# Hybrid RG-LRU / attention block: the first two chunk pairs of the MLP's first product as eight plain products each, sums of squares off POOL

## Chip, core and metric

One core of a Trainium2 chip runs the whole program in one launch. The metric is device time in microseconds, the median of three runs.

## What is computed

A transformer block on 512 tokens of width 1024, in float32: RMS norm, a fused input projection, a gated linear recurrence (RG-LRU) beside differential attention, a gated merge, and then the part that matters here:

```python
x = x + merged @ w_out[l]
h2 = rms_norm(x, norm2_g[l])
x = x + jnp.square(jax.nn.relu(h2 @ w_mlp1[l])) @ w_mlp2[l]
return rms_norm(x, normf_g)
```

w_mlp1 is 1024 x 4096, w_mlp2 is 4096 x 1024.

## The kernel before

**Layout and precision.** Activations lie transposed, 128 features on the partitions and 512 tokens along a row. A float32 product is made of three float32r products: each operand is split into a rounded part ("hi") and the remainder ("lo"), and hi*hi, hi*lo and lo*hi are summed in PSUM. A split is a cast on ScalarE (ACT) and a subtraction on VectorE (DVE): `part` (L132, L133) for whole weight chunks, `split_to` (L191 to L193) for everything in the MLP.

**w_out (L710 to L739).** Eight products, one for each 128 output features, of 24 matmuls with 512 columns (`mm`, L163 to L165), in the order m = 0, 4, 1, 5, 2, 6, 3, 7 (`OUT_ORDER`); n counts them. After each, DVE adds the residual (L719, tile E) and scales by the gain (L722, tile V; halves m and m+4 of a pair k = m % 4 lie in one tile), ACT squares (L724, L727) and POOL adds the squares to `ssq` (L728). The token mean itself is not applied to the activation: it is folded into x2 (L752) and into the final norm, so that the MLP need not wait for it.

**The MLP's first product.** It is cut into four quarters q of the hidden width, each of four chunk pairs i: one unit `("one", q, i)` makes hidden features i and i + 4 of quarter q (256 in all) for all 512 tokens. A unit is a 2 x 2 block product (input features in halves, tokens in halves of 256), done with seven products in place of eight (the Strassen-Winograd scheme): `one` (L777 to L799) uses the activation quarters b11, b21, b22 and four combinations t1 to t4, and seven weight pieces, four of which are sums of raw weight blocks (L206 to L211, DVE). Each of the seven products is 12 matmuls of 256 columns (`mm4`, L237) into one of four half banks BX, BY, BR, BZ. DVE and ACT read these partial results in between (L785, L787, L789, L791, L793, L795, L797); then `f_split` (L766) squares the relu and splits it into the tiles V and B (q even) or R and Q (q odd).

The activation combinations t1 to t4 are formed for each k when m = k + 4 is done (L734 to L738: two subtractions, one addition, one subtraction, then a split of 1024 columns), and the plain quarters b11 (tiles S0, S1) and b21, b22 (tiles L) are split there too.

**The MLP's second product.** Units `("two", q, i)` (L801) take two output features m of the hidden quarter q: 48 matmuls with 512 columns, added to x2 by L808.

**Order.** The four units (one, 0, 0..3) come first, alone; then `one` of the next quarter and `two` of this one alternate (`mlp_order`, L69). Weight pieces pass through a ring of eight (`RING`, L168): `use(n)` (L228) makes the split of piece n + 7 before it hands out piece n, and 2, 4, 6 and 8 of them are asked for during and behind w_out (L713, L740). SP loads one unit's raw weights (1 MB) ahead (`load_unit`, L185, two buffers). The framework sets the order in which each engine takes its instructions before the program runs, by dependences and the program's order; on an engine it isn't always the program's. Behind w_out also stand the token sums (`token_sums`, L329, on PE), a few small DVE instructions (L743 to L748), a broadcast on PE (L336), its copy on ACT (L340) and the scaling of x2 (L752, four of 128 x 1024).

Of the kernel before, what the change touches and what calls it, by code (L numbers as in the profile page):

```python
# [9 lines left out]
FR = mybir.dt.float32r  # L10
AF = mybir.ActivationFunctionType
ALU = mybir.AluOpType
AX = mybir.AxisListType

P = 128
T = 512
# [3 lines left out]
NQ = 4  # L20
# [17 lines left out]
H2 = T // 2  # L38
# [30 lines left out]
def mlp_order():  # L69

    order = [("one", 0, i) for i in range(4)]
    for q in range(NQ):
        for i in range(4):
            if q + 1 < NQ:
                order.append(("one", q + 1, i))
            order.append(("two", q, i))
    return order


def merge_order():  # L80
# [8 lines left out]
class Build:  # L89
# [12 lines left out]
    def t(self, tag, shape=(P, T), dt=F, bufs=1):  # L102
        self.n += 1
        return self.sb.tile(list(shape), dt, tag=tag, name=f"{tag}_{self.n}", bufs=bufs)

    def ps(self, tag, shape=(P, T), bufs=1):
        self.n += 1
        return self.pp.tile(list(shape), F, tag=tag, name=f"p{tag}_{self.n}", bufs=bufs)
# [61 lines left out]
    def plan_pieces(self):  # L170
        self.units = mlp_order()
        self.pieces = []
        self.first = []
        for u, (kind, q, i) in enumerate(self.units):
            self.first.append(len(self.pieces))
            if kind == "one":
                self.pieces += [(u, j) for j in range(7)]
            elif q < NQ - 1:
                self.pieces += [(u, j) for j in range(4)]
        self.ring_h, self.ring_l = [], []  # L180
        self.piece, self.made = {}, 0
        self.raw_u = {}
        self.sums = {}
# [11 lines left out]
    def make_piece(self):  # L195
        V, n = self.nc.vector, self.made
        u, j = self.pieces[n]
        self.load_unit(u)
        self.load_unit(u + 1)
        raw = self.raw_u[u]  # L200
        blk = [raw[:, i] for i in range(4)]
        if self.units[u][0] == "one":

            if j == 0:
                s1 = self.sums[u] = self.t("pT", (P, T))
                V.tensor_tensor(s1, blk[2], blk[3], op=ALU.add)  # L206
                V.tensor_tensor(blk[2], blk[2], blk[0], op=ALU.add)
            elif j == 1:
                V.tensor_tensor(blk[0], blk[0], self.sums[u], op=ALU.add)
            elif j == 6:  # L210
                V.tensor_tensor(blk[1], blk[1], blk[0], op=ALU.add)  # L211
            src = (blk[0], blk[0], blk[2], self.sums[u], blk[1], blk[3], blk[1])[j]
        else:
            src = blk[j]
        s, e = n // 2 % (self.RING // 2), n % 2
        if n < self.RING and e == 0:
            self.ring_h.append(self.t("whi", (P, 2, T), FR, bufs=4))
            self.ring_l.append(self.t("wlo", (P, 2, T), FR, bufs=4))
        hi, lo = self.ring_h[s][:, e], self.ring_l[s][:, e]
        self.split_to(src, hi, lo)  # L220
        self.piece[n] = [x.rearrange("p (k m) -> p k m", m=P) for x in (hi, lo)]
        self.made += 1
# [6 lines left out]
        self.make_until(n + self.RING)  # L229
        return self.piece.pop(n)  # L230

    def mm4(self, out, w, xs, first, last):

        nc = self.nc
        for k, (xh, xl) in enumerate(xs):
            for g, (l, r) in enumerate(((w[0], xh), (w[0], xl), (w[1], xh))):
                nc.tensor.matmul(out, l[:, k], r, start=(first and k == 0 and g == 0),  # L237
                                 stop=(last and k == 3 and g == 2), skip_group_check=True)

    def proj(self, xh, xl):  # L240
# [7 lines left out]
def block_kernel(ctx: ExitStack, tc: tile.TileContext, a):  # L248
    nc = tc.nc
    b = Build(tc, ctx, a)  # L250
    b.cur = 0
    t, ps = b.t, b.ps
    V, A, TE = nc.vector, nc.scalar, nc.tensor
# [39 lines left out]
    last = [None]  # L293
# [12 lines left out]
    def col(off, i):  # L306
        return sm[:, off + i:off + i + 1]
# [25 lines left out]
    def bcast_rinv(r, out, sl=range(4)):  # L333
        pb = ps("tr", (P, T))
        for i in sl:
            TE.matmul(pb[:, i * P:(i + 1) * P], r[:, i:i + 1].to_broadcast([P, P]), ident, start=True, stop=True)  # L336
        if out is None:
            return pb
        s = slice(sl[0] * P, (sl[-1] + 1) * P)
        A.copy(out[:, s], pb[:, s])  # L340

    def pair(tag):
        p = t(tag, (P, 2, T), FR)
        return p[:, 0], p[:, 1]
# [11 lines left out]
    ssq = t("up1")  # L356
# [12 lines left out]
    for half in range(2):  # L369
        for kp in range(4):  # L370
# [7 lines left out]
            for kk in range(2):  # L378
                k = 2 * kp + kk
# [23 lines left out]
                for n, (xs, wi) in enumerate(((xh, 0), (xl, 0), (xh, 1))):  # L403
                    for q, i in todo:
                        TE.matmul(pvs[half][i], xs[q][:, i * P:(i + 1) * P], (hv, lv)[wi][:, q % 2],  # L405
                                  start=(q == 0 and n == 0), stop=(q == KT - 1 and n == 2))
# [217 lines left out]
    for j in range(KT // 2):  # L624
        for n in range(8):
            s = 8 * j + n
            p_ = b.proj(xh, xl)
            h = 2 * j + n // 4
# [74 lines left out]
    x2, x2p = [None] * KT, [None] * (KT // 2)  # L703
    th = [t(f"X{2 * k}", (P, 4, H2), FR) for k in range(4)]
    tl = [t(f"X{2 * k + 1}", (P, 4, H2), FR) for k in range(4)]
    b2h = [t(f"L{k}", (P, 2, T), FR) for k in range(2)]
    b2l = [t(f"L{k + 2}", (P, 2, T), FR) for k in range(2)]
    b1h, b1l = t("S0", (P, 4, H2), FR), t("S1", (P, 4, H2), FR)
    ssq = t("up1")
    for n, m in enumerate(OUT_ORDER):  # L710
        k = m % 4
        if n > 4:
            b.make_until(2 * (n - 4))  # L713
        if x2p[m // 2] is None:
            x2p[m // 2] = t(f"E{m // 2}", (P, 2, T))
        xk = x2[m] = x2p[m // 2][:, m % 2]
        nc.sync.dma_start(xk, a["xT"][m])
        po = b.proj(mh, ml)
        V.tensor_tensor(xk, po, xk, op=ALU.add)  # L719
        if m < 4:  # L720
            xs = t(f"V{k}", (P, 2, T))
        V.scalar_tensor_tensor(xs[:, m // 4], xk, col(C_G2, m), r1b, op0=ALU.mult, op1=ALU.mult)  # L722
        if n == 0:
            A.activation(ssq, xk, AF.Square)  # L724
        else:
            sq = t("tmp", bufs=2)
            A.activation(sq, xk, AF.Square)  # L727
            nc.gpsimd.tensor_tensor(ssq, ssq, sq, op=ALU.add)  # L728
        if m >= 4:

            q4 = xs.rearrange("p a (c f) -> p (a c) f", c=2)
            b.split_to(q4[:, 0], b1h[:, k], b1l[:, k])

            tt = t(f"B{k}", (P, 4, H2))  # L734
            V.tensor_tensor(tt[:, 0:3:2], q4[:, 0:2], q4[:, 1:4:2], op=ALU.subtract)
            V.tensor_tensor(tt[:, 1], tt[:, 0], q4[:, 3], op=ALU.add)
            V.tensor_tensor(tt[:, 3], q4[:, 2], tt[:, 1], op=ALU.subtract)
            b.split_to(tt, th[k], tl[k])  # L738
            b.split_to(xs[:, 1], b2h[k // 2][:, k % 2], b2l[k // 2][:, k % 2])  # L739
    b.make_until(b.RING)  # L740
    pc = token_sums([ssq])
# [4 lines left out]
    eps4 = t("eps4", (P, 4))  # L746
    V.tensor_tensor(eps4, sig2, sig2, op=ALU.mult)
    V.tensor_scalar(eps4, eps4, EPS, None, op0=ALU.mult)  # L748
    sg2b = t("up0")
    bcast_rinv(sig2, sg2b)  # L750
    for xp in x2p:
        V.tensor_tensor(xp, xp, sg2b.unsqueeze(1).to_broadcast([P, 2, T]), op=ALU.mult)  # L752


    xc = {
        "b11": [(b1h[:, k], b1l[:, k]) for k in range(4)],
        "b21": [(b2h[k // 2][:, k % 2, :H2], b2l[k // 2][:, k % 2, :H2]) for k in range(4)],
        "b22": [(b2h[k // 2][:, k % 2, H2:], b2l[k // 2][:, k % 2, H2:]) for k in range(4)],
    }
# [4 lines left out]
    fq = {q: [None] * KT for q in range(NQ)}  # L764

    def f_split(q, f, z, lo_half):  # L766
        if q % 2 == 0:
            hi, lo = pair(f"V{f}" if f < 4 else f"B{f - 4}")
        else:
            hi, lo = pair(f"R{f}" if f < 4 else f"Q{f - 4}")  # L770
        A.activation(z[:, lo_half:], z[:, lo_half:], AF.Relu)
        A.activation(hi, z, AF.Square)
        A.activation(z, z, AF.Square)
        V.tensor_tensor(lo, z, hi.bitcast(F), op=ALU.subtract)
        fq[q][f] = (hi, lo)

    def one(u, q, i):  # L777
        n = b.first[u]
# [21 lines left out]

    def two(u, q, i):  # L801
        n = b.first[u]
        for c in range(2):
            m = 2 * i + c
            pz = ps("mm", bufs=3)
            for h in range(2):
                b.mm4(pz, b.use(n + 2 * c + h), fq[q][4 * h:4 * h + 4], h == 0, h == 1)
            V.tensor_tensor(x2[m], pz, x2[m], op=ALU.add)  # L808
# [15 lines left out]

    held = 0
    for u, (kind, q, i) in enumerate(b.units):
        if kind == "one":
            one(u, q, i)
        elif q < NQ - 1:
            two(u, q, i)  # L830
            if q == NQ - 2 and i >= 2:
                hold(len(b.units) - 4 + held, held)
                held += 1
# [5 lines left out]
    ssq = t("up1")  # L839
    for half in range(2):  # L840
        s = slice(half * H2, (half + 1) * H2)
        for m in range(KT):
            hi, lo = last_chunks[m]
            pz = ps("mm", bufs=3)
# [4 lines left out]
            sq = t("tmp", bufs=2)  # L849
# [5 lines left out]
        c = slice(2 * half, 2 * half + 2)  # L855
# [6 lines left out]
        for m, w in ((0, 1), (1, 1), (2, 2), (4, 2), (6, 2)):  # L862
            xp = x2p[m // 2][:, m % 2:m % 2 + w, s]
# [75 lines left out]
```

## Time and profile before

| | us |
|---|---|
| median of three runs | 908.75 (908.32 to 909.1) |
| the profiled execution | 908.68 |
| its span | 906.9 |
| PE busy | 885.7 (98%) |
| DVE busy | 597.1 (66%) |
| ACT busy | 477.5 (53%) |
| POOL busy | 11.7 (1%) |

The span is from the first to the last instruction; 1.8 us lie around it. PE is TensorE's matmuls, PEld its weight loads, which overlap them; matmuls are pipelined, so the recorded duration of one overlaps that of the next, and the pace is read from start to start. The same holds for DVE: in a dense run the starts of 512-wide instructions stand closer than their durations say. Some matmul records can be missing. The granted clock is a share of full speed: 1.00 is 2.4 GHz and 0.50 is 1.2 GHz. psc and pmm are tiles of PSUM; X, S, L, V, B, E, R and Q are tiles of SBUF as above; whi and wlo are the weight ring.

### The profile page before, as it was taken

Reading aid. Unit: us, or ns where it says so; the run is one execution under the profiler, and the core shown is the slowest. Engines: PE = TensorE matmul, PEld = TensorE weight load, DVE = VectorE, ACT = ScalarE, POOL = GpSimd, SP = SyncE. Lnnn points to the kernel's source line nnn. Section 1 sums busy time; section 2 is a strip of 40 time slices with the busy share of each in tenths; the row PEclk is TensorE's granted clock in tenths of the full one; section 3 lists DMA queues with packets and bytes.
Section 4 is the critical chain, followed back from the end, with each engine's and each line's share of the span. In section 5 each row is a group of like instructions: output and inputs, shape, how many; then the busy total and the mean of one; then the engine's idle time right before and its main releaser. Section 6 shows DMA issues by size and latency. Waiting matters only on the chain.

```text
span 906.9 us, 12306 instructions
## 1 busy us (share of the span) xinstructions
PE 885.7 (98%) x4793; PEld 741.9 (82%) x4793; DVE 597.1 (66%) x1008; ACT 477.5 (53%) x863; POOL 11.7 (1%) x12
## 2 busy tenths in 40 slices
PE   9999999999999999999999987999999999999996
PEld 7887777777877788888888877888888888888996
DVE  7767697787787765333334998776666666665633
ACT  7634767857758974222223344664444444445532
POOL 0000000000000000000000210000000000000000
PEclk9999999999999999999999978999999999999998
DMA  8443123133222112222522211222333222233211
GB/s 295 145 134 112 58 70 128 59 111 100 93 83 92 43 53 91 93 94 93 186 93 93 94 47 47 94 94 94 101 115 110 93 93 94 94 102 124 100 48 46
DMA packets 20745, 88.58 MB, mean 98 GB/s; under 512 B 3024, under 2 KB 6352, under 8 KB 11728
## 3 DMA queue, kind: packets, MB, share of 16 engines
q1 hardware_dynamic: 20688, 87.81, 28.3%
q8 instruction: 37, 0.61, 0.3%
q14 instruction: 20, 0.16, 0.1%
HBM read 81.51 MB, written 2.10 MB: 92 GB/s over the span
## 4 chain that ended last, share of the span: by engine, by line
PE 92%; DVE 5%; ACT 2%; issue 1%; POOLq 0%; DVEq 0%; ACTq 0%
PE pmm L237 20%; PE psc L237 17%; PE pmm L163 14%; PE pmm L165 14%; PE pmm L164 14%; PE pmm L405 3%; PE psc L405 2%; PE psc L493 2%; PE pmm L528 2%; PE ptr L516 1%; DVE wlo L193 1%; DVE V L722 1%; PE psc L589 1%; ACT whi L192 1%; PE ptr L336 1%
## 5 line engine op out<-in xcount | busy, mean ns | idle before, releaser
L192 ACT CAST whi<-raw 128x512 fp32r<-128x512 f32 (+1 forms) x148 | 90.5, 629 | 135.6 <-PE psc L237 59.3
L132 ACT CAST whi<-raw 128x1024 fp32r<-128x1024 f32 (+1 forms) x76 | 76.3, 1006 | 130.9 <-PE pmm L164 121.4
L163 PE MATMUL pmm<-X,whi 128*128 128x512 f32 x328 | 132.4, 404 | 0.0
L164 PE MATMUL pmm<-X,whi 128*128 128x512 f32 x328 | 130.1, 397 | 0.0
L165 PE MATMUL pmm<-X,wlo 128*128 128x512 f32 x328 | 130.0, 396 | 0.0
L133 DVE TENSOR_TENSOR wlo<-raw,whi 128x1024 fp32r<-128x1024 f32 (+1 forms) x76 | 89.5, 1179 | 60.0 <-ACT whi L132 59.4
L193 DVE TENSOR_TENSOR wlo<-raw,whi 128x512 fp32r<-128x512 f32 (+1 forms) x148 | 103.7, 709 | 33.3 <-ACT whi L192 30.7
L237 PE MATMUL psc<-X,whi 128*128 128x256 f32 x512 | 99.2, 292 | 1.7 <-ACT tmp L785 1.0
L237 PEld LDWEIGHTS psc<-X,whi 128*128 128x128 f32 x512 | 81.3, 194 | 7.6 <-DVE rot L791 2.0
L163 PEld LDWEIGHTS pmm<-X,whi 128*128 128x128 f32 x328 | 61.7, 188 | 18.1 <-issue 2.6
L165 PEld LDWEIGHTS pmm<-X,wlo 128*128 128x128 f32 x328 | 61.7, 188 | 15.0
L164 PEld LDWEIGHTS pmm<-X,whi 128*128 128x128 f32 x328 | 61.8, 188 | 14.3 <-issue 0.4
L237 PE MATMUL psc<-X,wlo 128*128 128x256 f32 x256 | 71.4, 286 | 0.0
L237 PE MATMUL psc<-L,whi 128*128 128x256 f32 x256 | 51.0, 294 | 7.1 <-DVE tmp L787 7.1
L237 PEld LDWEIGHTS psc<-L,whi 128*128 128x128 f32 x256 | 39.9, 191 | 13.6 <-DVE tmp L787 10.1
L237 PEld LDWEIGHTS psc<-X,wlo 128*128 128x128 f32 x256 | 48.8, 194 | 0.0
L297 ACT ACTIVATE B<-psc,nb 128x128 f32<-128x128 f32 (+3 forms) x64 | 33.2, 523 | 26.8 <-DVE nb L498 23.9
L297 ACT ACT_TABLE_LOAD x32 | 41.1, 1283 | 1.1 <-DVE nb L498 0.5
L237 PE MATMUL pmm<-V,whi 128*128 128x512 f32 x128 | 41.6, 396 | 0.0
L237 PE MATMUL pmm<-B,whi 128*128 128x512 f32 x128 | 40.0, 394 | 0.0
L237 PE MATMUL psc<-L,wlo 128*128 128x256 f32 x128 | 36.3, 283 | 0.0
L237 PE MATMUL pmm<-R,whi 128*128 128x512 f32 (+1 forms) x128 | 32.2, 335 | 0.0
(306 smaller groups left out, 1858.7 us busy)
## 6 DMA issues: line engine op xcount, KB each, us to landing
raw<-wts SPq DMA_DIRECT2D x70, 1024.0 KB, 4.8
rot<-B SPq DMA_DIRECT2D x64, 64.0 KB, 2.0
L<-xT SPq DMA_DIRECT2D x8, 256.0 KB, 5.3
raw<-wts SPq DMA_DIRECT2D x8, 256.0 KB, 5.3
E<-xT SPq DMA_DIRECT2D x8, 256.0 KB, 5.2
out<-E SPq DMA_DIRECT2D x6, 256.0 KB, 2.5
tmp<-gates SPq DMA_DIRECT2D x8, 128.0 KB, 4.6
out<-E SPq DMA_DIRECT2D x4, 128.0 KB, 1.9
```

What stands on the lines that cost most here:

```text
L132: nc.scalar.copy(hf[:, s], raw[:, s])
L133: nc.vector.tensor_tensor(lf[:, s], raw[:, s], hf[:, s].bitcast(F), op=ALU.subtract)
L163: nc.tensor.matmul(ps, hi[:, k], xh[k], start=(k == 0), stop=False)
L164: nc.tensor.matmul(ps, hi[:, k], xl[k], start=False, stop=False)
L165: nc.tensor.matmul(ps, lo[:, k], xh[k], start=False, stop=(k == KT - 1))
L192: self.nc.scalar.copy(hi, src)
L193: self.nc.vector.tensor_tensor(lo, src, hi.bitcast(F), op=ALU.subtract)
L237: nc.tensor.matmul(out, l[:, k], r, start=(first and k == 0 and g == 0), stop=(last and k == 3 and g == 2), skip_group_check=True)
L297: ins = A.activation(*args, **kw).ins
L405: TE.matmul(pvs[half][i], xs[q][:, i * P:(i + 1) * P], (hv, lv)[wi][:, q % 2], start=(q == 0 and n == 0), stop=(q == KT - 1 and n == 2))
L493: TE.matmul(sc[:, m, :n], l[rows, 0, i * P:n], r[rows, 1, :n], start=(g == 0), stop=(g == 2))
L528: TE.matmul(po[:, i], pdT[:, j], v[j][:, h * P:(h + 1) * P], start=(j == 0), stop=(j == i))
```

## The change

The units (one, 0, 0) and (one, 0, 1) are done with eight plain products instead of seven: `one_plain` multiplies the four raw weight blocks with the activation quarters b11, b12, b21 and b22 (b12 is split for it, tiles B0 and B1), into whole banks "mm", two halves of 256 columns each, of which the first matmul alone clears the bank. These two units have four weight pieces each and no weight sums. The combinations t1 to t4 move into `combine(k)`, called twice behind each of the two units. The sums of squares run on DVE. The scaling of x2 moves to the start of the first four second products. The tiles of even and odd quarters change places.

```diff
--- before.py
+++ after.py
@@ -77,6 +77,11 @@
     return order
 
 
+def plain(q, i):
+
+    return q == 0 and i < 2
+
+
 def merge_order():
     order = [("gr", m) for m in range(4)] + [("w_br_rnn", m) for m in range(4)]
     for m in range(KT):
@@ -173,9 +178,9 @@
         self.first = []
         for u, (kind, q, i) in enumerate(self.units):
             self.first.append(len(self.pieces))
-            if kind == "one":
+            if kind == "one" and not plain(q, i):
                 self.pieces += [(u, j) for j in range(7)]
-            elif q < NQ - 1:
+            elif kind == "one" or q < NQ - 1:
                 self.pieces += [(u, j) for j in range(4)]
         self.ring_h, self.ring_l = [], []
         self.piece, self.made = {}, 0
@@ -199,7 +204,7 @@
         self.load_unit(u + 1)
         raw = self.raw_u[u]
         blk = [raw[:, i] for i in range(4)]
-        if self.units[u][0] == "one":
+        if self.units[u][0] == "one" and not plain(*self.units[u][1:]):
 
             if j == 0:
                 s1 = self.sums[u] = self.t("pT", (P, T))
@@ -229,12 +234,12 @@
         self.make_until(n + self.RING)
         return self.piece.pop(n)
 
-    def mm4(self, out, w, xs, first, last):
+    def mm4(self, out, w, xs, first, last, clear=None):
 
         nc = self.nc
         for k, (xh, xl) in enumerate(xs):
             for g, (l, r) in enumerate(((w[0], xh), (w[0], xl), (w[1], xh))):
-                nc.tensor.matmul(out, l[:, k], r, start=(first and k == 0 and g == 0),
+                nc.tensor.matmul(out, l[:, k], r, start=((first if clear is None else clear) and k == 0 and g == 0),
                                  stop=(last and k == 3 and g == 2), skip_group_check=True)
 
     def proj(self, xh, xl):
@@ -706,6 +711,8 @@
     b2h = [t(f"L{k}", (P, 2, T), FR) for k in range(2)]
     b2l = [t(f"L{k + 2}", (P, 2, T), FR) for k in range(2)]
     b1h, b1l = t("S0", (P, 4, H2), FR), t("S1", (P, 4, H2), FR)
+    b12h, b12l = t("B0", (P, 4, H2), FR), t("B1", (P, 4, H2), FR)
+    q4s = []
     ssq = t("up1")
     for n, m in enumerate(OUT_ORDER):
         k = m % 4
@@ -725,17 +732,13 @@
         else:
             sq = t("tmp", bufs=2)
             A.activation(sq, xk, AF.Square)
-            nc.gpsimd.tensor_tensor(ssq, ssq, sq, op=ALU.add)
+            V.tensor_tensor(ssq, ssq, sq, op=ALU.add)
         if m >= 4:
 
             q4 = xs.rearrange("p a (c f) -> p (a c) f", c=2)
+            q4s.append(q4)
             b.split_to(q4[:, 0], b1h[:, k], b1l[:, k])
-
-            tt = t(f"B{k}", (P, 4, H2))
-            V.tensor_tensor(tt[:, 0:3:2], q4[:, 0:2], q4[:, 1:4:2], op=ALU.subtract)
-            V.tensor_tensor(tt[:, 1], tt[:, 0], q4[:, 3], op=ALU.add)
-            V.tensor_tensor(tt[:, 3], q4[:, 2], tt[:, 1], op=ALU.subtract)
-            b.split_to(tt, th[k], tl[k])
+            b.split_to(q4[:, 1], b12h[:, k], b12l[:, k])
             b.split_to(xs[:, 1], b2h[k // 2][:, k % 2], b2l[k // 2][:, k % 2])
     b.make_until(b.RING)
     pc = token_sums([ssq])
@@ -746,14 +749,23 @@
     eps4 = t("eps4", (P, 4))
     V.tensor_tensor(eps4, sig2, sig2, op=ALU.mult)
     V.tensor_scalar(eps4, eps4, EPS, None, op0=ALU.mult)
+
+    def combine(k):
+
+        q4 = q4s[k]
+        tt = t(f"B{2 + k % 2}", (P, 4, H2))
+        V.tensor_tensor(tt[:, 0:3:2], q4[:, 0:2], q4[:, 1:4:2], op=ALU.subtract)
+        V.tensor_tensor(tt[:, 1], tt[:, 0], q4[:, 3], op=ALU.add)
+        V.tensor_tensor(tt[:, 3], q4[:, 2], tt[:, 1], op=ALU.subtract)
+        b.split_to(tt, th[k], tl[k])
+
     sg2b = t("up0")
     bcast_rinv(sig2, sg2b)
-    for xp in x2p:
-        V.tensor_tensor(xp, xp, sg2b.unsqueeze(1).to_broadcast([P, 2, T]), op=ALU.mult)
 
 
     xc = {
         "b11": [(b1h[:, k], b1l[:, k]) for k in range(4)],
+        "b12": [(b12h[:, k], b12l[:, k]) for k in range(4)],
         "b21": [(b2h[k // 2][:, k % 2, :H2], b2l[k // 2][:, k % 2, :H2]) for k in range(4)],
         "b22": [(b2h[k // 2][:, k % 2, H2:], b2l[k // 2][:, k % 2, H2:]) for k in range(4)],
     }
@@ -764,15 +776,28 @@
     fq = {q: [None] * KT for q in range(NQ)}
 
     def f_split(q, f, z, lo_half):
-        if q % 2 == 0:
+        if q % 2:
             hi, lo = pair(f"V{f}" if f < 4 else f"B{f - 4}")
         else:
             hi, lo = pair(f"R{f}" if f < 4 else f"Q{f - 4}")
-        A.activation(z[:, lo_half:], z[:, lo_half:], AF.Relu)
+        if lo_half < T:
+            A.activation(z[:, lo_half:], z[:, lo_half:], AF.Relu)
         A.activation(hi, z, AF.Square)
         A.activation(z, z, AF.Square)
         V.tensor_tensor(lo, z, hi.bitcast(F), op=ALU.subtract)
         fq[q][f] = (hi, lo)
+
+    def one_plain(u, q, i):
+        n = b.first[u]
+        for c in range(2):
+            pz = ps("mm", bufs=3)
+            for h in range(2):
+                w = b.use(n + 2 * c + h)
+                for e in range(2):
+                    b.mm4(pz[:, e * H2:(e + 1) * H2], w, xc[f"b{h + 1}{e + 1}"], h == 0, h == 1, h == e == 0)
+            z = t(f"up{2 + c}" if i % 2 == 0 else "rot", bufs=1 + i % 2)
+            A.activation(z, pz, AF.Relu)
+            f_split(q, i + 4 * c, z, T)
 
     def one(u, q, i):
         n = b.first[u]
@@ -800,6 +825,8 @@
 
     def two(u, q, i):
         n = b.first[u]
+        if q == 0:
+            V.tensor_tensor(x2p[i], x2p[i], sg2b.unsqueeze(1).to_broadcast([P, 2, T]), op=ALU.mult)
         for c in range(2):
             m = 2 * i + c
             pz = ps("mm", bufs=3)
@@ -824,7 +851,11 @@
 
     held = 0
     for u, (kind, q, i) in enumerate(b.units):
-        if kind == "one":
+        if kind == "one" and plain(q, i):
+            one_plain(u, q, i)
+            combine(2 * i)
+            combine(2 * i + 1)
+        elif kind == "one":
             one(u, q, i)
         elif q < NQ - 1:
             two(u, q, i)
```

## Rows read from the trace of the kernel before

**Rows 1.** The page: busy time by engine; granted clock in 40 slices (tenths).
```profile
PE 885.7 (98%) x4793; PEld 741.9 (82%) x4793; DVE 597.1 (66%) x1008; ACT 477.5 (53%) x863; POOL 11.7 (1%) x12
...
PEclk9999999999999999999999978999999999999998
```

**Rows 2.** Busy time by stretch: each engine's us (count), granted clock, DMA share, GB/s.
```profile
502.00:529.10 27.10, 27.10 (x120) 22.24 (x119) 25.28 (x34) 12.04 (x18) 6.52 (x4) 1.00 0.15 56
...
529.10:549.00 19.90, 10.90 (x53) 9.67 (x52) 18.34 (x28) 7.38 (x14) 2.59 (x2) 0.68 0.15 54
...
596.75:618.10 21.35, 21.35 (x134) 18.95 (x133) 15.29 (x27) 10.27 (x20) 0.00 (x0) 1.00 0.29 99
```

**Rows 3.** Order of time on PE: start us, us, operation, count, [idle before <-releaser].
```profile
523.40 0.39 PE L165 MATMUL pmm<-Q,wlo 128*128 128x512 f32 x1
...
528.90 0.39 PE L165 MATMUL pmm<-Q,wlo 128*128 128x512 f32 x1
...
532.28 0.38 PE L237 MATMUL psc<-S,whi 128*128 128x256 f32 x1 [1.93 <-ACT S L192]
...
549.00 0.80 PE L237 MATMUL psc<-L,whi 128*128 128x256 f32 x2 [4.97 <-DVE tmp L787]
...
550.53 0.41 PE L237 MATMUL psc<-X,wlo 128*128 128x256 f32 x1
...
552.45 0.41 PE L237 MATMUL psc<-X,wlo 128*128 128x256 f32 x1
...
562.21 0.28 PE L237 MATMUL psc<-L,wlo 128*128 128x256 f32 x1
...
564.34 0.28 PE L237 MATMUL psc<-X,wlo 128*128 128x256 f32 x1
```

**Rows 4.** Order of time on DVE, same columns, around the end of w_out.
```profile
522.77 0.75 DVE L722 SCALAR_TENSOR_TENSOR V<-E,small,up 128x512 f32<-128x512 f32 x1
...
525.14 0.68 DVE L735 TENSOR_TENSOR B<-V 128x512 f32<-128x512 f32 x1
...
525.74 0.68 DVE L193 TENSOR_TENSOR L<-V,L 128x512 fp32r<-128x512 f32 x1
...
526.35 0.41 DVE L736 TENSOR_TENSOR B<-B,V 128x256 f32<-128x256 f32 x1
...
526.68 0.68 DVE L206 TENSOR_TENSOR pT<-raw 128x512 f32<-128x512 f32 x1
...
528.22 0.68 DVE L719 TENSOR_TENSOR E<-pmm,E 128x512 f32<-128x512 f32 x1
...
528.82 1.22 DVE L193 TENSOR_TENSOR X<-B,X 128x1024 fp32r<-128x1024 f32 x1
...
529.95 1.83 DVE L722 SCALAR_TENSOR_TENSOR V<-E,small,up 128x512 f32<-128x512 f32 x1
...
533.85 0.68 DVE L719 TENSOR_TENSOR E<-pmm,E 128x512 f32<-128x512 f32 x1
...
543.98 4.63 DVE L752 TENSOR_TENSOR E<-E,up 128x1024 f32<-128x1024 f32 x4 [1.35 <-ACT up L340]
```

**Rows 5.** Order of time on POOL, the sixth sum of squares.
```profile
529.97 1.27 POOL L728 TENSOR_TENSOR up<-up,tmp 128x512 f32<-128x512 f32 x1 [5.30 <-ACT tmp L727]
```

**Rows 6.** Busy time by stretch of line L237 alone: PE, PEld, clock, DMA.
```profile
529.10:596.75 67.65, 52.80 (x372) 49.16 (x372) 0.87 0.22 79
...
529.10:561.80 32.70, 20.30 (x120) 18.54 (x119) 0.74 0.18 65
...
561.80:573.80 12.00, 10.96 (x84) 10.22 (x84) 1.00 0.26 89
...
585.80:596.75 10.95, 10.59 (x84) 10.18 (x85) 1.00 0.28 98
```

**Rows 7.** Line L336 by operation: duration ns min/median/max, first and last start.
```profile
L336 PE MATMUL ptr<-ident,isz x8: 271/275/275, 484.3 to 485.1; 128*128 128x128 f32 x8
```

**Rows 8.** Order of time on ACT, one 512-wide cast.
```profile
536.05 0.62 ACT L192 CAST L<-V 128x512 fp32r<-128x512 f32 x1
```

## Prediction

> **What bounds the kernel now.** I read the page first: TensorE (PE) is busy for 98% of the span, so only PE's own time counts, and the row of granted clocks has one dip in its middle [rows 1]. Next the busy times by stretch, around that dip [rows 2]: up to 529.1 us (the eight w_out products) PE is full; from 529.1 to 549.0 it is busy for 10.90 of 19.90 us, at a mean clock of 0.68. VectorE (DVE) is the full engine there: 25.28 of 27.10 us, then 18.34 of 19.90.
>
> Then PE's order of time [rows 3]. The last w_out matmul starts at 528.90. The MLP's first products begin behind it, wait for S (the split quarter b11) until 532.28, and from 544 to 549.00 for DVE's L787. What a half-clock stretch costs stands in the same rows: from 550.53 to 552.45 nine matmuls of 256 columns start (0.213 us each), from 562.21 to 564.34 eighteen (0.118 us each). So the lower of the two clock levels (1.2 GHz) nearly doubles each matmul, and it was granted where PE had stood idle.
>
> Last DVE's order of time [rows 4], which tells why PE waits. The x2 addition of the seventh product (n=6, m=3), whose last matmul starts at 523.40, begins at 528.22; that of the last product begins at 533.85, although the product was complete at 528.90 + 0.39 = 529.29: DVE is 4.6 us behind. Everything b11, t1 to t4 and b2 need comes through this queue. Between these two additions stand an activation combination (L735, L736) and its 1024-wide split (528.82), weight sums (L206), and an L722 of 1.83 us which is 0.75 us elsewhere. It started at 529.95, while POOL's sum of squares ran from 529.97 for 1.27 us [rows 5]. Each of the seven POOL sums has one such stretched DVE instruction beside it. At the end the four x2 scalings (L752) hold L787, for which PE waits until 549.00, from 543.98 to 548.6.
>
> **What the stretch costs.** From 529.1 to 596.75, where the second product of the MLP begins, 372 L237 matmuls are recorded [rows 6]; at 0.118 us they are 43.9 us. The eight broadcast records before w_out took 484.3 to 485.1 and some 0.3 us more [rows 7], about 0.9 us; the token sums have eight records too, for which I estimate as much: 1.8 us. So 67.65 - 43.9 - 1.8 = 22.0 us are lost: up to 561.8 with 120 matmuls 32.70 - 14.2 - 1.8 = 16.7, then 2.1 in each of two units (12.00 for 84 x 0.118 = 9.9) and 1.0 in the last (10.95).
>
> **The change, part by part.**
> *Two units with eight plain products.* Each has 96 matmuls of 256 columns instead of 84: 24 more in all, 24 x 0.118 = +2.8 us on PE, all on the path. Here two halves of one bank are filled in turn; the trace has no such pair. Its pace is bounded below by the dense 0.118 (same shape, same weight loads, full clock, so no gain) and above by 12.00/84 = 0.143, the pace of a unit with its waits (+4.8 us over 192 matmuls). I take 0.118, as nothing is read from the bank before it is complete.
>
> *DVE's queue ahead of the first product.* Start to start, a 512-wide DVE instruction takes 0.60 us, a 1024-wide split 1.13 (528.82 to 529.95), a 256-wide one at most 0.41 [rows 4]. A combination is 0.60 + 2 x 0.41 + 1.13 = 2.55 us. Ahead of the addition at 533.85 leave three combinations (7.65), six weight sums (6 x 0.60 = 3.6, one of them stands in the rows; the plain units split raw weights) and five POOL overlaps at 1.83 - 0.75 = 1.08 each (5.4). There come six sums of squares on DVE (3.6) and three to four b12 splits (4 x 0.41 = 1.6). Net -11.5 us against a backlog of 4.6: the backlog goes, and DVE follows the products as they end. ACT loses four 1024-wide casts and gains four 256-wide ones, no load. The ring holds eight splits before the first unit as it did.
>
> POOL's sums are bounded as DVE work by 0 (if they fit into DVE's gaps) and 7 x 0.60 = 4.2; I take the full 4.2 in the net above, since each is queued in front of a split. The Trainium skill's Perfetto Trace Analysis, section Optimizing Scalar/DVE Operations, says that with a saturated DVE moving work to another engine, GpSimd among them, may make sense, and adds that the port shared by the two may undo it. Read as a rule it speaks against this part: the 5.4 us would not come back, the net would be -6.1, a margin of 1.5 over the backlog instead of 6.9, and where that is used up the time would be rival B's. The stretched L722 starts 0.02 us from a POOL sum and outlasts it [rows 4, 5]; I keep the larger net.
>
> *The first product's waits.* The new first bank needs b11 and b12 first, both from m=0 to 3, so from the product whose last matmul starts at 523.40: with no backlog they are split at 523.79 + 0.69 + 0.75 + 0.62 + 2 x 0.41 = 526.7 (an addition, L722, a cast, two splits). These 24 matmuls cover 2.8 us after 529.13. Then b21 and b22 with k=3 are due, from the last product: 529.29 + addition 0.69 + L722 0.75 + an ACT cast of 0.62 [rows 8] + split 0.68 = 532.0, against 531.96; nine matmuls of the k=0 to 2 parts stand in front (1.06 us). Bounds: 0, and one 1.13 us instruction that happens to hold DVE plus the last sum of squares, 1.7 us; I take 0.5, as the cover is there in either order. With no long idle time the clock should stay at the full level (2.4 GHz), as it did to 529.1 [rows 2]. Token sums and broadcast stay on PE (1.8 us), with slack: their result is next needed in the second product.
>
> *Combinations behind the plain units.* 4 x 2.55 = 10.2 us of DVE and four wide casts on ACT, now beside 192 x 0.118 = 22.7 us of PE work. In these DVE also has seven weight splits (4.2), four weight sums (2.4), four square remainders (2.4) and the late part of the last token tile (about 3): 22.2 us against 22.7, tight if nothing is done earlier; but the tiles of k=0 to 2 are complete during w_out, where DVE gets room (-11.5), and the trace shows that an engine's order is not the program's (the weight sum L206, for the MLP, runs between L736 and the seventh product's L719). I cost it at 0, bounds 0 to 4 (it arrives late by what doesn't fit, about one and a half combinations), cover: the two plain units.
>
> *Scalings of x2.* L752's four (1.16 us each in its 4.63) leave the queue before L787 and stand in the first four second products. There DVE is busy 15.29 of 21.35 us [rows 2]: cost taken 0.5, bounds 0 and 4.6. The q-even results now lie in R and Q: nothing added, these tiles were last read by w_out, over when the first result is written. SP's loads of raw weights wait for the splits of an earlier unit; with four splits instead of seven they go out earlier.
>
> **The sum.** Before, the stretch from 529.13 to the third unit's point of the pattern is 561.80 + 12.00 = 573.80 [rows 6], 44.7 us. After, it holds 192 + 36 = 228 matmuls: 26.9 + 1.8 + first wait 0.5 + 0.5 for the wait for L787 that each pattern of seven has = 29.7. Gain 15.0, less 0.5 for the scalings: 14.5. The rest (units three and four, 12.0 and 10.95) keeps its losses. The profiled execution took 908.68 us (span 906.9 and 1.8 around it), 0.07 under the median of 908.75: forecast 908.75 - 14.5 = 894.2. A measurement of this kernel can tell about 0.2% (1.8 us) from no change.
>
> **Rivals.**
> A. *Units three and four run dense too* (their splits run ahead while DVE and ACT have room): up to 2.1 + 1.0 more, 891. For: the plain units need three splits fewer each. Against: the pattern's own waits on L787 recur in all three units before. Chance 0.10.
> B. *The queue stays late*, because combinations of k=0 to 2 are hoisted in front of the last splits after all (the change does not do what it says), or because the stretched instructions had another cause than POOL: PE idles, the clock falls, and about half of the 14.5 is left: 901. For: such hoisting is seen [rows 4]. Against: the margin of 6.9. Chance 0.12. [...]
> C. *Combinations late for unit three*: it waits up to 4 us for t1 to t4, 898. Chance 0.13.
> D. *Slower*: PE's list has the token sums ahead of the first products, and these need DVE's last sum of squares, which stands at the end of its queue. If DVE's queue is as late as before, PE stands before the token sums as long as it stood before b11 and L787; the 16.7 us stay and 2.8 are added: 911.5. It decides once DVE's last addition starts later than 533.85. Against: -11.5. Chance 0.03.
>
> **Chances and range.** Forecast 0.62, with A to D as above. Range: the forecast's own is 892.5 to 897; with A and C it reaches from 890 to 900, which leaves B and D outside (0.15) and holds the bounds of the scalings (898.3) and of the first wait (895.4). Faster by over 0.2%: 0.96 (all but D and 0.01); within 0.2%: 0.01, if the 22 us only move; slower: 0.03.
>
> **What would show it.** Right: L719 of the last product starts by 530; the clock row has no dip; PE is idle for under 2 us between w_out and the third unit; the third unit's L787 falls near 559; DVE instructions of 512 columns never take over 0.8 us in w_out. Wrong in the first step: an idle PE with a clock of 0.5 behind w_out. Wrong in the third: PE waiting for a split from L735's tile at 552. Wrong in the last: DVE's x2 scaling ahead of the second product's addition, with PE waiting for a bank.

## The result and the profile after

The changed kernel takes 893.5 us (median of four) against 908.88 before: ratio 0.983, 95% interval 0.9811 to 0.9849. Three of the four executions took 893.03 to 893.68 us at a mean granted clock of 0.996 to 0.998, the fourth took 1221.54 us at 0.654, for a reason that no trace shows, and the ratio leaves it out. Forecast were 894.2, range 890 to 900.

The page of the changed kernel: span, busy time, granted clock. They answer to [rows 1].

```profile
span 891.2 us, 12316 instructions
...
PE 879.4 (99%) x4817; PEld 737.9 (83%) x4817; DVE 582.0 (65%) x995; ACT 474.3 (53%) x857; POOL 0.3 (0%) x5
...
PEclk9999999999999999999999999999999999999998
```

The dip of the clock is gone. Busy times by stretch (PE, PEld, DVE, ACT, POOL, then clock, DMA), answering to [rows 2]:

```profile
502.00:529.10 27.10, 27.10 (x121) 22.25 (x120) 25.60 (x41) 13.83 (x25) 0.00 (x0) 1.00 0.28 103
...
529.10:549.00 19.90, 19.90 (x170) 19.81 (x170) 18.91 (x33) 11.11 (x19) 0.00 (x0) 1.00 0.16 54
...
549.00:561.80 12.80, 12.56 (x103) 12.06 (x102) 8.47 (x15) 7.40 (x15) 0.00 (x0) 1.00 0.25 82
```

PE is now busy for all of the 19.90 us behind w_out, where it was for 10.90, and DVE as full ahead of it as before (25.60 of 27.10 us, with 41 instructions for 34). PE's order of time, answering to [rows 3]:

```profile
528.70 0.39 PE L170 MATMUL pmm<-Q,wlo 128*128 128x512 f32 x1
...
528.93 0.40 PE L242 MATMUL pmm<-S,whi 128*128 128x256 f32 x2
...
531.84 1.02 PE L334 MATMUL ptr<-ones,up 128*128 128x1 f32 x8
...
532.72 0.49 PE L242 MATMUL pmm<-L,whi 128*128 128x256 f32 x2
...
535.29 1.05 PE L341 MATMUL ptr<-ident,sig 128*128 128x128 f32 x8
...
536.10 0.48 PE L242 MATMUL pmm<-L,whi 128*128 128x256 f32 x2
```

Behind the last w_out matmul the plain products start 0.23 us later, at the pace of the row. Token sums (531.84 to 532.72) and broadcast (535.29 to 536.10) stand between them, and PE waits for neither. DVE's order of time, answering to [rows 4]:

```profile
498.24 1.22 DVE L138 TENSOR_TENSOR wlo<-raw,whi 128x1024 fp32r<-128x1024 f32 x1
...
504.19 0.69 DVE L735 TENSOR_TENSOR up<-up,tmp 128x512 f32<-128x512 f32 x1
...
521.82 0.69 DVE L757 TENSOR_TENSOR B<-V 128x512 f32<-128x512 f32 x1
...
523.64 0.69 DVE L726 TENSOR_TENSOR E<-pmm,E 128x512 f32<-128x512 f32 x1 [0.21 <-PE pmm L170]
...
524.85 0.75 DVE L729 SCALAR_TENSOR_TENSOR V<-E,small,up 128x512 f32<-128x512 f32 x1
...
527.99 1.22 DVE L198 TENSOR_TENSOR X<-B,X 128x1024 fp32r<-128x1024 f32 x1
...
529.13 0.69 DVE L726 TENSOR_TENSOR E<-pmm,E 128x512 f32<-128x512 f32 x1
...
537.00 1.23 DVE L829 TENSOR_TENSOR E<-E,up 128x1024 f32<-128x1024 f32 x1 [0.91 <-ACT up L345]
...
557.42 0.42 DVE L812 TENSOR_TENSOR tmp<-psc,tmp 128x256 f32<-128x256 f32 x1
...
569.29 0.42 DVE L812 TENSOR_TENSOR tmp<-psc,tmp 128x256 f32<-128x256 f32 x1
...
580.79 0.42 DVE L812 TENSOR_TENSOR tmp<-psc,tmp 128x256 f32<-128x256 f32 x1
```

The last product's x2 addition (now L726) starts at 529.13, 0.04 us behind its product (528.70 + 0.39), where DVE was 4.6 us late. L138 and L735 show the plain durations (1.22 and 0.69 us). The first L812 (old L787) is that of the third unit: 557.42, before 573.38. So 16.0 us are gained there; at the end of the span 906.9 - 891.2 = 15.7 are left. From the first plain product to the end of this L812 PE never stands, and all 228 matmuls and the 16 small ones are recorded:

```profile
528.93:557.84 28.91, 28.90 (x244) 28.60 (x243) 23.77 (x40) 16.82 (x29) 0.00 (x0) 1.00 0.22 74
```

### The profile page after: what moved, and what is told of

It reads as the page before. It is cut to its first block, busy times and chain, and to the rows that moved or that the text cites. A ratio compares the mean times of both kernels' runs of the same rounds, so it can differ in the third digit from the quotient of the medians.

```text
span 891.2 us, 12316 instructions
## 1 busy us (share of the span) xinstructions
PE 879.4 (99%) x4817; PEld 737.9 (83%) x4817; DVE 582.0 (65%) x995; ACT 474.3 (53%) x857; POOL 0.3 (0%) x5
## 4 chain that ended last, share of the span: by engine, by line
PE 96%; DMA 1%; DVE 1%; ACT 1%; issue 0%; SPq 0%; DVEq 0%; ACTq 0%
PE pmm L242 22%; PE pmm L168 16%; PE pmm L170 15%; PE pmm L169 15%; PE psc L242 15%; PE psc L410 2%; PE psc L498 2%; PE pmm L410 2%; PE pmm L533 2%; PE ptr L521 1%; DMA raw<-wts 1%; PE psc L594 1%; DMA L<-xT 1%; PE ptr L341 0%; PE psc L596 0%
## 5 line engine op out<-in xcount | busy, mean ns | idle before, releaser
L138 DVE TENSOR_TENSOR wlo<-raw,whi 128x1024 fp32r<-128x1024 f32 (+1 forms) x76 | 88.4, 1164 | 60.2 <-ACT whi L137 59.6
L242 PE MATMUL psc<-X,whi 128*128 128x256 f32 x448 | 84.1, 286 | 0.6 <-DVE up L816 0.2
L242 PEld LDWEIGHTS psc<-X,whi 128*128 128x128 f32 x448 | 69.0, 188 | 5.9 <-DVE up L816 1.7
L242 PE MATMUL psc<-X,wlo 128*128 128x256 f32 x224 | 60.8, 280 | 0.0
L242 PE MATMUL psc<-L,whi 128*128 128x256 f32 x224 | 43.7, 291 | 1.7 <-DVE tmp L812 1.7
L242 PEld LDWEIGHTS psc<-X,wlo 128*128 128x128 f32 x224 | 41.3, 188 | 0.0
L242 PE MATMUL pmm<-R,whi 128*128 128x512 f32 x128 | 41.1, 392 | 0.0
L242 PEld LDWEIGHTS psc<-L,whi 128*128 128x128 f32 x224 | 34.3, 188 | 7.4 <-DVE tmp L812 4.3
L242 PE MATMUL pmm<-Q,whi 128*128 128x512 f32 x128 | 39.7, 391 | 0.0
L242 PE MATMUL pmm<-B,whi 128*128 128x256 f32 (+1 forms) x160 | 37.5, 325 | 0.0
L242 PE MATMUL pmm<-V,whi 128*128 128x512 f32 (+1 forms) x128 | 32.4, 338 | 0.0
```

The costliest lines, as they stand in the source:

```text
L138: nc.vector.tensor_tensor(lf[:, s], raw[:, s], hf[:, s].bitcast(F), op=ALU.subtract)
L242: nc.tensor.matmul(out, l[:, k], r, start=((first if clear is None else clear) and k == 0 and g == 0), stop=(last and k == 3 and g == 2), ...
```

## Experiments

Twelve kernels, each timed beside the kernel before on the same chip (there 908.3 to 908.8 us). First the changed kernel with one part undone or altered.

**Sums of squares on POOL again.**

```diff
-            V.tensor_tensor(ssq, ssq, sq, op=ALU.add)
+            nc.gpsimd.tensor_tensor(ssq, ssq, sq, op=ALU.add)
```

> The changed kernel with the seven sums of squares on POOL again. Theory (POOL's overlap makes DVE's queue late): each of the last five sums stretches one DVE instruction by 1.08 us and takes 0.60 us of adds off DVE, so DVE is later by up to 5 x 0.48 = 2.4 us at the last product, less the short gaps that it has in the changed kernel; the split of b21 and b22 and the token sums, which PE takes up at 531.8 and 532.7, come 1 to 3 us late and PE stands that long: 894.5 to 897, possibly with a dip of the clock. Rival (the plain units alone cover any lateness of DVE, since 24 matmuls stand in front): 893.5, within 0.9.

900.68 us (899.8 to 901.21; ratio to before 0.9895 to 0.9925): 7.2 us slower than the changed kernel, above the theory's range and far from the rival. DVE, then PE, then busy times by stretch of this run:

```profile
525.66 0.68 DVE L726 TENSOR_TENSOR E<-pmm,E 128x512 f32<-128x512 f32 x1
...
532.97 0.68 DVE L726 TENSOR_TENSOR E<-pmm,E 128x512 f32<-128x512 f32 x1
```

```profile
531.45 0.38 PE L242 MATMUL pmm<-S,whi 128*128 128x256 f32 x1 [0.55 <-DVE S L198]
...
536.09 1.36 PE L334 MATMUL ptr<-ones,up 128*128 128x1 f32 x8 [3.32 <-POOL up L735]
```

```profile
528.90:536.00 7.10, 3.32 (x23) 2.79 (x21) 7.07 (x10) 2.99 (x6) 2.48 (x2) 1.00 0.00 0
...
536.00:544.00 8.00, 7.91 (x41) 7.91 (x42) 4.22 (x12) 1.20 (x2) 0.04 (x1) 0.57 0.39 134
...
544.00:552.00 8.00, 8.00 (x70) 8.00 (x70) 7.94 (x10) 5.41 (x9) 0.00 (x0) 1.00 0.00 0
```

The addition of the seventh product starts 2.0 us later than in the changed kernel, that of the last 3.8 us. PE's list has the token sums behind the first 24 matmuls, so PE stands 3.32 us for the last POOL sum, and then runs at a mean clock of 0.57 for 8 us. The waits (0.55 and 3.32) and an estimate for the clock, 8.00 x (1 - 0.57) = 3.4, make 7.3 us. The direction was the theory's; the size was not: it had 2.4 us of lateness, and no figure for the clock.

**POOL additions that nobody needs.**

```diff
+    scr = t("up3")
...
             V.tensor_tensor(ssq, ssq, sq, op=ALU.add)
+            nc.gpsimd.tensor_tensor(scr, sq, sq, op=ALU.add)
```

> The changed kernel, its sums of squares on DVE, with seven POOL additions put beside them (each square added to itself, written to a tile that nobody reads; no other engine's order changes, and nobody waits for POOL's result). Theory (a POOL addition holds up the DVE instruction beside it): seven DVE instructions take about 1.1 us longer, the last product's L726 starts 2 to 5 us late, and PE waits before the token sums with the clock falling: 898 to 902. Rival (the 7.2 us of the run with POOL's sums came from waiting for POOL's own slow additions): DVE's durations stay and the time is 893.5 within 0.9.

897.9 us (895.82 to 899.89), 0.1 us under the theory's range and clear of the rival. DVE and ACT take their instructions in the order of the changed kernel, and nobody waits for POOL. DVE, POOL and PE:

```profile
498.35 2.06 DVE L138 TENSOR_TENSOR wlo<-raw,whi 128x1024 fp32r<-128x1024 f32 x1
...
504.98 1.53 DVE L736 TENSOR_TENSOR up<-up,tmp 128x512 f32<-128x512 f32 x1
...
532.35 0.68 DVE L727 TENSOR_TENSOR E<-pmm,E 128x512 f32<-128x512 f32 x1
```

```profile
497.79 1.54 POOL L737 TENSOR_TENSOR up<-tmp 128x512 f32<-128x512 f32 x1 [496.96 <-ACT tmp L735]
...
504.29 1.67 POOL L737 TENSOR_TENSOR up<-tmp 128x512 f32<-128x512 f32 x1 [4.96 <-ACT tmp L735]
...
521.66 3.70 POOL L737 TENSOR_TENSOR up<-tmp 128x512 f32<-128x512 f32 x1 [4.43 <-ACT tmp L735]
...
533.89 3.10 POOL L737 TENSOR_TENSOR up<-tmp 128x512 f32<-128x512 f32 x1 [5.03 <-ACT tmp L735]
```

```profile
535.03 1.02 PE L334 MATMUL ptr<-ones,up 128*128 128x1 f32 x8 [2.72 <-DVE up L736]
```

The split L138 at 498.35 takes 2.06 us instead of 1.22, the sum L736 at 504.98 1.53 instead of 0.69, each beside a POOL addition; the last addition starts at 532.35 instead of 529.13, and PE stands 2.72 us before the token sums. So POOL's running alone slows DVE, without any wait for POOL's result: the theory's way holds in this, and the part of rival B that doubted it falls. Two details missed: the seven stretches are 0.68 to 0.84 us, not 1.1, and in the profiled execution the clock did not fall. Of the 7.2 us of the run with POOL's sums, 4.4 come back with idle additions (medians); the other 2.8 are not taken apart, but there the token sums also wait for the last POOL sum itself. That POOL's running slows DVE is what the Trainium skill's SBUF — State Buffer (section SBUF: two separate sides) states: DVE instructions with two SBUF inputs and GpSimd share a port that one of them holds alone; the trace agrees, with these durations, and in both directions, as POOL's fifth and seventh additions took 3.70 and 3.10 us against 1.29 to 1.67 for the other five.

**Scalings of x2 at their old place.**

```diff
     bcast_rinv(sig2, sg2b)
+    for xp in x2p:
+        V.tensor_tensor(xp, xp, sg2b.unsqueeze(1).to_broadcast([P, 2, T]), op=ALU.mult)
```

(and the scaling taken out of `two`)

> The changed kernel with the four scalings of x2 at their old place, directly behind the broadcast. Theory (their place matters only where a partial result waits on DVE behind them, and the plain units have none): they take 4.6 us of DVE in one go while PE has plain products to do, 893.5 within 0.9. Rival (their place ahead of everything else was a main share of the old stall): a new wait of 2 to 5 us on PE, 895.5 to 898.5.

893.94 us (892.94 to 895.84): no difference. The theory holds: the four run from 537.12 for 4.63 us, while PE has plain products.

**Combinations in the w_out loop.**

```diff
             b.split_to(q4[:, 1], b12h[:, k], b12l[:, k])
+            combine(k)
```

(and both calls behind the plain units taken out)

> The changed kernel with each combination formed in the w_out loop, ahead of the split of b2, as before; everything else as changed. Theory (three of the four combinations run during w_out in the changed kernel anyway, so only that of k=3 comes forward): DVE has 2.5 us more ahead of the last split of b2, PE waits 0 to 2 us there: 893.5 to 895.5. Rival (forming them behind the plain units is what takes the stall away, as the prediction's -7.65 us had it): the backlog of 4.6 us is back, 897 to 901.

893.9 us (893.76 to 894.43): no difference to speak of. Where the program forms them decides little, as three of four run during w_out in either kernel (L757 at 499.97, 510.96 and 521.82 in the changed one).

**Only the plain units kept**: all three of the edits above together.

> The changed kernel with only the plain units kept: sums on POOL, combinations in the w_out loop, scalings behind the broadcast, all as before. Theory (of the three, only POOL's sums cost anything in this kernel): as the run with POOL's sums alone, 900.7, from 899.5 to 902. Rival (the parts cover each other, and DVE's queue with all three is as late as before): 904 to 909.

899.66 us (899.25 to 900.06): as the theory has it. PE stands at the same place, for the same time:

```profile
535.04 1.44 PE L334 MATMUL ptr<-ones,up 128*128 128x1 f32 x8 [3.31 <-POOL up L745]
```

**The number of plain units.** One (`q == 0 and i < 1`, four combinations behind it), then four (`q == 0`):

> Only the first unit plain, all four combinations behind it (12 matmuls fewer than in the changed kernel). Theory (one plain unit already covers DVE's late tail; a second unit of seven costs 11.9 us instead of 11.3): 893.5 plus 0.6, from 893 to 895. Rival (the fourth combination, of k=3, is not ready behind one unit of 11.3 us, and PE waits for t2 to t4 with the clock falling): 896 to 900.

893.33 us (892.26 to 894.17): the second plain unit is worth nothing that can be told; one covers DVE's tail, and the theory's time holds. Its way does not: the second unit, now of seven, takes 10.84 us, and it is the last of the four that is dear (12.34; L812 to L812).

> All four first units plain (the third and fourth too, 24 matmuls more), combinations behind the first two units. Theory (a unit of seven that stands alone costs 11.9 and 11.5 us because of its waits on DVE, a plain one 96 x 0.118 = 11.3): 0.8 us less, 892.7, from 892 to 893.5. Rival (the extra matmuls count in full, as the waits only move to the next unit): 893.5 + 2.8 = 896.3.

896.53 us (896.09 to 896.76): the rival's number, but the first units themselves don't show its way. The fifth unit's L812 comes at 580.21, 0.58 us earlier than in the changed kernel (580.79), as the theory had it. The next pair gives that back (601.97 against 601.65). Later, from 666 to 711 us, two pairs take 22.58 and 22.61 us where the changed kernel's take 21.60. The waits of that stretch (us in total, times, longest), and the row on DVE ahead of the first late L812, here and in the changed kernel:

```profile
PE psc L242 <- DVE tmp L812: 1.9, 2, 1.0
```

```profile
688.43 0.69 DVE L211 TENSOR_TENSOR pT<-raw 128x512 f32<-128x512 f32 x1 [1.78 <-DMA raw<-wts]
```

```profile
686.52 0.69 DVE L211 TENSOR_TENSOR pT<-raw 128x512 f32<-128x512 f32 x1 [0.41 <-DMA raw<-wts]
```

DVE's order in these pairs is the same in both. What differs is the load of raw weights: L211 waits for it, L812 stands behind L211, and PE waits for L812. From issue to landing the load takes 6.0 us here and 4.7 in the changed kernel. Why is not shown, and it is not bound to four plain units: the changed kernel has one such load itself, further on (its pair from 773.59 to 796.04 takes 22.45 us). So the late loads explain 1 us net; the last scaling of the output starts 1.6 us later than in the changed kernel (886.58 against 884.98), and the other 1.7 us of the profiled execution lie behind it, where the output is written. How much of the 3.0 us the extra matmuls cost stays open.

**The kernel before with single parts.** Sums on DVE alone; scalings moved alone; both.

```diff
-            nc.gpsimd.tensor_tensor(ssq, ssq, sq, op=ALU.add)
+            V.tensor_tensor(ssq, ssq, sq, op=ALU.add)
```

> The kernel before with its sums of squares on DVE and nothing else changed. Theory (POOL's additions are the main cause of the late queue, 3 to 4 us in the run with dummy additions): the last product's x2 addition starts within 1.5 us of the product's end, PE's first waits shrink, the wait for L787 behind the scalings stays: 901 to 904. Rival (DVE is full in any case, and seven sums of 0.60 us cost it what POOL's overlap gave back; the gain of the pair came from the scalings): 907 to 909.

> The kernel before with the four scalings of x2 at the head of the second products and nothing else changed. Theory (the 4.97 us wait for L787 behind them goes, with the half clock that follows it): 902 to 905. Rival (the scalings only stand where DVE waits anyway; with POOL's sums the queue is as late as before and PE stands elsewhere): 907 to 909.

> The kernel before with two parts of the change and without the plain units: the sums of squares on DVE, the scalings of x2 at the head of the second products. Theory (each is worth much by itself, since the wait for L787 behind the scalings and the late queue are what PE stands for): the 4.97 us wait and the half clock behind it go (about 7), the queue is some 2.4 us earlier: 898 to 901. Rival (without the plain units PE still waits for t2, t3 and t1 of k=3 and for partial results, and the clock falls once more): 902 to 906.

898.38 (897.79 to 898.46), 902.82 (902.18 to 903.68) and 897.7 us (897.35 to 898.13). The sums alone give 10.4 us, more than the theory's 5 to 8; the scalings 6.0, as expected; both together hardly more than the sums, 0.3 us under the theory's range.

Why the sums alone give so much: ahead of the addition at 533.85 six DVE instructions of the kernel before are stretched, each beside a POOL sum, by 1.08 to 1.12 us. One is in [rows 4]; the others:

```profile
498.90 1.78 DVE L735 TENSOR_TENSOR B<-V 128x512 f32<-128x512 f32 x1
...
505.00 2.32 DVE L133 TENSOR_TENSOR wlo<-raw,whi 128x1024 fp32r<-128x1024 f32 x1
...
511.43 1.79 DVE L735 TENSOR_TENSOR B<-V 128x512 f32<-128x512 f32 x1
...
516.87 1.87 DVE L722 SCALAR_TENSOR_TENSOR V<-E,small,up 128x512 f32<-128x512 f32 x1
...
523.43 1.78 DVE L193 TENSOR_TENSOR wlo<-pT,whi 128x512 fp32r<-128x512 f32 x1
```

With the sums on DVE and nothing else changed, the last x2 addition starts right behind its product (528.47 + 0.39 = 528.86). PE's last w_out matmul and that addition in this run:

```profile
528.47 0.39 PE L165 MATMUL pmm<-Q,wlo 128*128 128x512 f32 x1
```

```profile
528.90 0.69 DVE L719 TENSOR_TENSOR E<-pmm,E 128x512 f32<-128x512 f32 x1
```

So the whole backlog of 4.6 us goes with POOL's sums alone. The theory's other half, that the wait for L787 behind the scalings stays, fails: behind 537 us no wait of PE is longer than 0.87 us. But PE still waits for the k=3 combination, and the clock falls; PE's order of time and one stretch of the same run:

```profile
535.06 0.62 PE L237 MATMUL psc<-X,whi 128*128 128x256 f32 x2 [1.45 <-ACT X L192]
...
536.45 0.58 PE L237 MATMUL psc<-X,whi 128*128 128x256 f32 x1 [0.77 <-DVE X L193]
```

```profile
535.00:544.00 9.00, 7.67 (x38) 7.16 (x38) 8.24 (x15) 3.55 (x8) 0.00 (x0) 0.62 0.27 107
```

With the scalings moved, the first wait stays and the wait of 4.97 us for L787 [rows 3] is 0.35 us (L785 there):

```profile
532.03 0.57 PE L237 MATMUL psc<-S,whi 128*128 128x256 f32 x1 [1.92 <-ACT S L192]
...
543.94 0.50 PE L237 MATMUL psc<-L,whi 128*128 128x256 f32 x2 [0.35 <-DVE tmp L785]
```

**A better order.** The first and third unit plain, or the first and fourth, four combinations behind the first:

```diff
-    return q == 0 and i < 2
+    return q == 0 and i in (0, 2)
```

> The first and the third unit plain instead of the first and the second; all four combinations behind the first. Theory (a unit of seven loses its 1.6 to 2 us because DVE and ACT cannot keep pace through two such units in a row; with a plain one between them they catch up): both units of seven lose half as much, 891.5 to 892.7. Rival (each unit of seven loses by its own chain of partial results, whatever stands beside it): 893.5 within 0.8.

> The first and the fourth unit plain, the second and third of seven products; all four combinations behind the first. Theory (as for the first and third: what costs is two units of seven in a row, and here they are in a row): 893.5 within 0.8. Rival (the last unit before the second products is the dear one, 12.3 us in the run with one plain unit against 10.8 and 11.2 for the two before it, so a plain one there saves): 891.8 to 892.8.

892.13 us (891.91 to 892.44) and 893.22 (892.93 to 893.62). The first is the fastest kernel of the study, 1.4 us under the changed one and 1.1 under the second, and the ranges do not overlap. Part of that lies ahead of the four units: the last w_out matmul of the profiled executions starts at 528.41, 529.19 and, in the changed kernel, 528.70. From there to the last scaling of the output they take 355.55, 356.25 and 356.28 us, so about 0.7 us belong to the order of the units. Busy times by stretch of the first: PE is full through all four units but for 0.1 us.

```profile
549.00:560.00 11.00, 11.00 (x94) 10.87 (x92) 9.91 (x17) 8.19 (x15) 0.00 (x0) 1.00 0.29 98
...
560.00:575.00 15.00, 14.95 (x123) 14.45 (x122) 9.46 (x17) 8.41 (x16) 0.00 (x0) 1.00 0.20 71
...
575.00:585.00 10.00, 9.95 (x77) 9.37 (x76) 7.98 (x15) 6.25 (x13) 0.00 (x0) 1.00 0.56 195
```

Both times lie in their theory's range and outside their rival's. That two units of seven in a row are what costs fits this; with 0.7 us and one profiled execution of each it is not shown beyond doubt.

## Why the prediction was right, step by step

- *The bound.* Right. PE's waits behind w_out and the half clock after them were the 16.7 us, and they are gone: 228 matmuls and the small records take 557.84 - 528.93 = 28.9 us, to the end of the first L812, against 29.7 forecast. The two waits of 0.5 each did not come; the pace was a little over 0.118. The signs named in advance came too: the addition at 529.13, no dip, no idle PE, the L812 at 557.42 for the 559.
- *Two plain units, +2.8 us.* Right: 192 matmuls at the dense pace; two halves of one bank cost nothing.
- *DVE's queue, net -11.5 us.* The step that failed. It had "Ahead of the addition at 533.85 leave three combinations (7.65)". None of the three left (the runs on the combinations, above), and of six weight sums five did (only L211 at 527.38 is ahead). Of the POOL overlaps it counted five, and there are six. So what left is 5 x 0.60 + 6 x 1.1 = 9.6 us; what came is six sums and three b12 splits, 3.6 + 1.2 = 4.8; net -4.8. Against a backlog of 4.6 that just suffices, where the prediction saw a margin of 6.9. That the time was hit all the same is in part luck: DVE cannot run ahead of the products, so more than the backlog can't be won there, and the 6.7 us too many did not show. The largest true term is POOL's, and the runs confirm it: without POOL's sums the backlog is gone even with everything else as before, and with POOL running it is back (3.8 us later than in the changed kernel with POOL's sums, 3.2 with idle additions).
- *POOL's sums, against the Trainium skill's Perfetto Trace Analysis, section Optimizing Scalar/DVE Operations.* The section says that with a saturated DVE moving work to another engine, GpSimd among them, may make sense, and that the port shared by the two may undo it. The prediction kept to its row against the first half, and was right; the second half is what the runs bear out: work taken off the full DVE onto POOL cost more than it freed, 10.4 us in the kernel before and 7.2 in the changed one.
- *First product's waits, 0.5 us.* None: the k=3 quarters came in time.
- *Combinations, cost 0.* Right, but for another reason than the cover by the plain units: they hardly moved.
- *Scalings, 0.5 us in the second products.* They run earlier than forecast, at 537.00 to 545.4 beside the plain units; cost 0.
- *Rivals.* A did not come: the third and fourth unit still take 11.87 and 11.50 us (L812 to L812). B's state is what the run with POOL's sums shows (900.7 for the 901). C and D did not come; D's place, PE before the token sums, is where PE stands in three of the runs, but for about 3 us, not 16.7, and not ahead of the first products but behind 24 of their matmuls.

What the single parts give does not add up: sums alone -10.4, scalings alone -6.0, plain units alone -8.7 (908.34 to 899.66), all together -15.4. They overlap, as each takes away some of the same stall. In the changed kernel only two are needed, POOL's sums off (7.2) and plain products (897.7 to 893.5: 4.2); the place of the combinations and of the scalings is worth nothing there. The exchange of the tiles of even and odd quarters goes with the plain units in every run and is not tested alone.

## What to carry to other kernels

Before work is moved to POOL to relieve a full DVE, look for DVE instructions of one shape with two durations, and lay POOL's rows beside them. Where the head of a stage depends on a chain (combinations, partial results), a little extra TensorE work without that chain, one unit of it, can be cheaper than the wait and the lower clock behind it. Setting such a unit between the dear ones rather than in a block gave the fastest kernel here, by about 1 us.

## Not expected of the hardware

The clock behind a wait does not follow from the length of the wait alone. With idle POOL additions the profiled execution had 2.72 us of waiting before the token sums and kept the full clock behind it (2.4 GHz):

```profile
535.00:544.00 9.00, 8.97 (x77) 9.00 (x78) 8.75 (x17) 4.79 (x8) 1.99 (x1) 1.00 0.33 118
```

The kernel before with its sums on DVE had shorter waits around the same time, 1.45 and 0.77 us, and its clock in the same stretch was 0.62 (its rows stand above), so part of it ran at the lower level (1.2 GHz). With POOL's sums the wait was 3.32 us and the clock fell to 0.57 behind it. What decides is not shown.

Nor does one program always get the same clock: with idle POOL additions the profiled execution took 895.82 us at a mean clock of 0.997, and three further executions took 897.52, 898.28 and 899.89 us at 0.995, 0.995 and 0.992. Only the first was profiled, so where the others lost clock is not recorded.
